# Attention scores with queries on partitions: row maxima and exponentials read from PSUM, probabilities transposed on TensorE

## The chip, the cores and the metric

The kernel runs on one NeuronCore of one Trainium2 chip. TensorE (PE) multiplies matrices, VectorE (DVE), ScalarE (ACT) and GpSimd (POOL) work element by element, and SyncE (SP) issues most of the DMAs. Each engine works through its own instruction list in order and waits on semaphores of the others. The metric is the device time of one execution in microseconds (us); lower is better. A change of about 0.2% is what measurements of this kernel can tell from none.

## The reference

One layer of an encoder on 256 prompt tokens and 1024 sample tokens: two branches (latent attention and a bidirectional retention), a gated merge, then an MLP. All in float32. The change touches the softmax attention, which has 8 heads, with 64 + 32 channels for the scores and 64 for the values:

```python
def block(args):
    qn, qr = args
    s = (jnp.einsum('bqhd,bkhd->bhqk', qn, k_nope)
         + jnp.einsum('bqhd,bkd->bhqk', qr, k_rope))
    p = jax.nn.softmax(s.astype(jnp.float32) * scale, axis=-1).astype(v.dtype)
    return jnp.einsum('bhqk,bkhd->bqhd', p, v)
...
a = mla_attention(q_nope, q_rope, k_nope, k_rope, v_a) @ w_branch_a
```

Prompt and sample tokens attend only among themselves, so a query has 256 or 1024 keys.

## The kernel before

All products are made in a split form: a float32 operand is written as a rounded high part (`split`, L55: a copy on ACT) and a low part (the difference, on DVE or POOL), and one product is three matmuls, high by high, high by low, low by high (`mm3`, L60). PSUM has eight banks of 128 x 512 floats, all taken from one pool (`psum`, L82). A scheduling layer lays the instructions of each engine out in one fixed order before the program is built; the order in which the code asks for work is its starting point.

The program goes through five stages: input projections, retention, attention (`phase_attn`, L640), merge (`phase_merge`) and MLP. During attention TensorE also has the gate projections to do, 16 x 3 groups of 8 products from the resident `hT` (generator `gates`, L646). They depend on nothing in the attention, and are dealt out between its steps as filler: `fill` (L792) takes as many as the share of attention done asks for, out of a total of `TOTF`; `PRE` (33) of them come ahead of the first scores, `ENDF` and `EL` are spent in the last rounds, and what is left runs at the start of the merge (`prep_o`, L842).

Attention is cut into 40 units, (head, 256 queries, all their keys): per head one unit with 2 key blocks of 128 and four with 8. The scores stand with keys on partitions and queries along the row. For a unit with 8 key blocks:

- `qk` (L697): 24 matmuls of 256 columns (the key block is the stationary operand), copied from PSUM into the SBUF tile `s` by ACT (L706).
- `kmax` (L709): DVE takes the maximum over the 8 key blocks, 2048 elements per partition (L711). `qmax1` (L714): two 128 x 128 transposes on TensorE and a second maximum on DVE (L720), `mc`. `qmax2` (L724): two more transposes (L727) spread the maximum of each query over all partitions, in PSUM.
- `soft` (L731): DVE subtracts it from `s` (L740), ACT takes the exponential (L742) and the high part `eh`; the low part `el` is made half by POOL, half by DVE. POOL adds up the blocks (L748) for the sums.
- `sums` (L755): two matmuls with a vector of ones finish the row sums, which go to DRAM (`l_s`).
- `av` (L764): 16 matmuls of 256 columns multiply with the values; DVE copies the result (L779) and SP stores it to `a_s`.

The main loop (L806) runs these as a pipeline over units: in one round the scores of unit i, the value product of unit i-3, the maxima of unit i-1, and so on. In the merge, `prep_a` (L1140) loads `l_s`, inverts it and stores `r_s`, from which the normalisation is broadcast. `load_o` (L857) loads the retention output into the tiles `ot`, which are transposed at the start of the merge (L104) before the first products with `w_branch_b`, whose raw weights come through `wload` (L145). `load_k` (L677) has one buffer: the keys of the next head are split once the last scores of this head are done.

Of the kernel before, what the change touches and what calls it, by code (L numbers as in the profile page):

```python
# [18 lines left out]
P = 128  # L19
# [19 lines left out]
TOTF = 13.25  # L39
ENDF = 8  # L40
PRE = 33
FA = 0.25
EB = (3, 5, 6, 7)
EL = 4
CK = 12
# [3 lines left out]
class Build:  # L49
# [104 lines left out]
    def build(self):  # L154
# [20 lines left out]
        self.l_s = d("l_s", [HEADS, T])  # L175
# [464 lines left out]
    def phase_attn(self):  # L640
# [47 lines left out]
        def load_q(u):  # L688
            h, s0, ns, q0 = u
            qraw = sp.tile([P, 256], F32, tag="qraw", name="qraw", bufs=1)  # L690
            nc.sync.dma_start(out=qraw, in_=self.q_s[h, :, q0:q0 + 256])
            qh = sp.tile([P, 256], F32R, tag="qh", name="qh")
            ql = sp.tile([P, 256], F32R, tag="ql", name="ql")
            self.split(qh, ql, qraw)
            return qh, ql

        def qk(u, q, k):  # L697
            h, s0, ns, q0 = u
            s = sp.tile([P, 8, 256], F32, tag="s", name="s", bufs=3)
            for i in range(0, ns, 2):  # L700
                ps = self.psum()
                for x in range(2):
                    kc = slice((s0 + i + x) * P, (s0 + i + x + 1) * P)
                    self.mm3(ps[:, x * 256:(x + 1) * 256], (k[0][:, kc], k[1][:, kc]), q,
                             True, True)
                nc.scalar.copy(s[:, i:i + 2], ps.rearrange("p (u n) -> p u n", u=2))  # L706
            return s

        def kmax(u, s):  # L709
            mx = sp.tile([P, 256], F32, tag="mx", name="mx")  # L710
            nc.vector.tensor_reduce(mx, s[:, 0:u[2]].rearrange("p k q -> p q k"), AX.X, ALU.max)  # L711
            return mx

        def qmax1(mx):  # L714
            ps = self.psum()
            for x in range(2):
                nc.tensor.transpose(out=ps[:, x * P:(x + 1) * P], in_=mx[:, x * P:(x + 1) * P],
                                    identity=self.ident)
            mc = sp.tile([P, 2], F32, tag="mc", name="mc")
            nc.vector.tensor_reduce(mc, ps[:, 0:256].rearrange("p (x k) -> p x k", x=2), AX.X,  # L720
                                    ALU.max)
            return mc

        def qmax2(mc):  # L724
            pb = self.psum()
            for x in range(2):
                nc.tensor.transpose(out=pb[:, x * P:(x + 1) * P],  # L727
                                    in_=mc[:, x:x + 1].broadcast_to([P, P]), identity=self.ident)
            return pb[:, 0:256]

        def soft(u, s, ma):  # L731
            h, s0, ns, q0 = u
            st = min(ns, 4)
            es = []
            for i in range((ns + 3) // 4):
                eh = sp.tile([P, 4, 256], F32R, tag="eh", name="eh", bufs=4)
                el = sp.tile([P, 4, 256], F32R, tag="el", name="el", bufs=4)
                es.append((eh, el))
                sv = s[:, 4 * i:4 * i + st]
                nc.vector.tensor_tensor(sv, sv, ma.unsqueeze(1).broadcast_to([P, st, 256]),  # L740
                                        ALU.subtract)
                nc.scalar.activation(sv, sv, AF.Exp, scale=SCALE)  # L742
                self.split(eh[:, 0:st], el[:, 0:st], sv, nc.vector if i else nc.gpsimd)
            n, src = ns, s
            t = sp.tile([P, 4, 256], F32, tag="t", name="t", bufs=1)
            while n > 1:
                n //= 2
                nc.gpsimd.tensor_tensor(t[:, 0:n], src[:, 0:n], src[:, n:2 * n], ALU.add)  # L748
                src = t
            sh = sp.tile([P, 256], F32R, tag="sh", name="sh", bufs=3)  # L750
            sl = sp.tile([P, 256], F32R, tag="sl", name="sl", bufs=3)
            self.split(sh, sl, t[:, 0])
            return es, (sh, sl)

        def sums(u, e):  # L755
            h, s0, ns, q0 = u
            pl = self.psum()[0:2, 0:256]
            for i in range(2):
                nc.tensor.matmul(pl, lhsT=one, rhs=e[1][1 - i], start=i == 0, stop=i == 1)
            lt = gt.tile([1, 256], F32, tag="lt", name="lt", bufs=1)  # L760
            nc.vector.tensor_copy(lt, pl[0:1])
            nc.sync.dma_start(out=self.l_s[h:h + 1, q0:q0 + 256], in_=lt)

        def av(u, v, e):  # L764
            h, s0, ns, q0 = u
            j = h % 2
            po = self.psum()[:, 0:256]
            for i in range(ns):
                eh, el = e[0][i // 4]
                if i == ns - 1:  # L770
                    nc.tensor.matmul(po[0:VD], lhsT=v[:, s0 + i, j, 0:VD], rhs=el[:, i % 4],
                                     start=False, stop=False)
                nc.tensor.matmul(po, lhsT=v[:, s0 + i, j], rhs=eh[:, i % 4], start=i == 0,
                                 stop=i == ns - 1)
                if i < ns - 1:
                    nc.tensor.matmul(po[0:VD], lhsT=v[:, s0 + i, j, 0:VD], rhs=el[:, i % 4],
# [29 lines left out]
        for i in range(nu + 4):  # L806
            if i + 1 < nu:
                q[i + 1] = load_q(units[i + 1])
# [687 lines left out]
```

## Time and profile before

| | us |
|---|---|
| median of 3 runs | 2189.68 (2186.43 to 2190.81) |
| the profiled execution, its own time | 2190.64 |
| its span in the trace | 2188.9 |

The profile is of that one execution. It names, for each engine, when an instruction ran, for how long, and what it had waited for. A matmul's duration includes the time until its result is in PSUM, and the next starts before it has ended; so what a matmul costs TensorE in a row of them is the distance from one start to the next, not its duration.

### The profile page before, as it was taken

What the parts mean: (1) busy time and instruction counts of PE and PEld (TensorE: products, weight loads), DVE (VectorE), ACT (ScalarE), POOL (GpSimd) and SP (SyncE); (2) the same over time, 40 slices, a digit from 0 to 9 for tenths busy, and PEclk for the clock granted to TensorE, in tenths of its full rate; (3) what the DMA queues carried; (4) which work ended last, traced back from release to release, by engine and by line L of the source; (5) the groups of instructions that cost most, each with busy time, mean ns of one, the idle gap of its engine ahead of it and who ended that gap; (6) DMA issues with size and microseconds to landing.
All of it is one profiled execution on the core that took longest, in us unless ns stands there. A gap on an engine that the chain in (4) does not pass through costs nothing.

```text
span 2188.9 us, 32539 instructions
## 1 busy us (share of the span) xinstructions
PE 2075.1 (95%) x11856; PEld 1802.5 (82%) x11856; DVE 1407.4 (64%) x2803; ACT 933.1 (43%) x1901; POOL 759.7 (35%) x574
## 2 busy tenths in 40 slices
PE   7899999999988899889899999799999989999998
PEld 6888989888977788777788899688888878878886
DVE  7744646464689898988423618765555545994558
ACT  6422222222366566566323524444444434433442
POOL 1212121211046566566224710244434414970110
PEclk8999999999999999999999999899999999999999
DMA  3351111110222323221554504143343357533444
GB/s 146 111 202 31 53 39 44 39 45 20 89 77 67 89 76 90 66 70 45 198 159 145 193 21 154 57 153 124 129 148 138 129 192 270 173 91 96 141 148 150
DMA packets 169569, 241.10 MB, mean 110 GB/s; under 512 B 15768, under 2 KB 104768, under 8 KB 169408
## 3 DMA queue, kind: packets, MB, share of 16 engines
q1 hardware_dynamic: 161408, 230.82, 32.4%
q10 hardware_dynamic: 8000, 8.20, 1.1%
q8 instruction: 93, 1.52, 0.3%
q14 instruction: 68, 0.56, 0.1%
HBM read 159.91 MB, written 79.05 MB: 109 GB/s over the span
## 4 chain that ended last, share of the span: by engine, by line
PE 73%; DVE 10%; issue 6%; ACT 4%; DMA 4%; POOL 3%; SPq 0%; DVEq 0%; ACTq 0%; POOLq 0%
PE ps L63 22%; PE ps L65 22%; PE ps L64 22%; POOL t L748 2%; ACT s L706 1%; DVE el L58 1%; PE ps L540 1%; PE ps L543 1%; DVE s L740 1%; DVE mx L711 1%; ACT s L742 1%; PE ps L521 1%; PE ps L586 1%; PE ps L585 1%; DVE ql L58 1%
## 5 line engine op out<-in xcount | busy, mean ns | idle before, releaser
L63 PE MATMUL ps<-wh,uh 128*128 128x512 f32 x550 | 209.3, 393 | 8.4 <-ACT wh L57 5.8
L64 PE MATMUL ps<-wl,uh 128*128 128x512 f32 x550 | 215.7, 392 | 0.0
L65 PE MATMUL ps<-wh,ul 128*128 128x512 f32 x550 | 215.1, 392 | 0.0
L58 DVE TENSOR_TENSOR ul<-ur,uh 128x640 fp32r<-128x640 f32 x110 | 123.8, 1125 | 114.4 <-ACT uh L57 114.3
L57 ACT CAST uh<-ur 128x640 fp32r<-128x640 f32 x110 | 80.4, 731 | 211.7 <-PE ps L64 168.1
L748 POOL TENSOR_TENSOR t<-s 128x1024 f32<-128x1024 f32 (+1 forms) x40 | 91.9, 2297 | 167.6 <-ACT s L742 109.7
L711 DVE TENSOR_REDUCE mx<-s 128x256 f32<-128x2048 f32 (+1 forms) x40 | 130.4, 3260 | 23.4 <-ACT s L706 23.2
L1203 POOL TENSOR_TENSOR a<-a 128x640 f32<-128x640 f32 x64 | 85.3, 1343 | 169.7 <-ACT a L1227 73.2
L63 PE MATMUL ps<-hTh,wgh 128*128 128x512 f32 (+1 forms) x384 | 141.5, 368 | 2.5 <-ACT s L706 1.6
L64 PE MATMUL ps<-hTl,wgh 128*128 128x512 f32 (+1 forms) x384 | 138.3, 360 | 0.0
L65 PE MATMUL ps<-hTh,wgl 128*128 128x512 f32 (+1 forms) x384 | 138.1, 360 | 0.0
L63 PEld LDWEIGHTS ps<-wh,uh 128*128 128x128 f32 x550 | 104.1, 189 | 31.0 <-ACT wh L57 9.2
L63 PE MATMUL ps<-wah,hTh 128*128 128x512 f32 x320 | 127.9, 400 | 0.0
L65 PE MATMUL ps<-wah,hTl 128*128 128x512 f32 x320 | 125.0, 391 | 0.0
L64 PE MATMUL ps<-wal,hTh 128*128 128x512 f32 x320 | 124.7, 390 | 0.0
L64 PEld LDWEIGHTS ps<-wl,uh 128*128 128x128 f32 x550 | 104.3, 190 | 22.4 <-DVE wl L58 0.6
L65 PEld LDWEIGHTS ps<-wh,ul 128*128 128x128 f32 x550 | 104.2, 190 | 21.7
L63 PE MATMUL ps<-h2h,feh 128*128 128x512 f32 (+1 forms) x352 | 117.8, 337 | 1.4 <-ACT h2h L57 1.4
L64 PE MATMUL ps<-h2l,feh 128*128 128x512 f32 (+1 forms) x352 | 118.5, 337 | 0.0
L58 POOL TENSOR_TENSOR el<-s,eh 128x1024 fp32r<-128x1024 f32 (+1 forms) x40 | 95.0, 2374 | 67.3 <-ACT eh L57 67.3
L65 PE MATMUL ps<-h2h,fel 128*128 128x512 f32 (+1 forms) x352 | 118.1, 337 | 0.0
L500 DVE TENSOR_TENSOR t<-ps,rcs 128x256 f32<-128x256 f32 x40 | 17.0, 424 | 154.0 <-ACT v L494 136.6
(343 smaller groups left out, 6582.7 us busy)
## 6 DMA issues: line engine op xcount, KB each, us to landing
u_s<-a SPq DMA_DIRECT2D x112, 320.0 KB
ur<-u_s SPq DMA_DIRECT2D x112, 320.0 KB
uraw<-w_up SPq DMA_DIRECT2D x32, 512.0 KB
wd<-w_down SPq DMA_DIRECT2D x64, 256.0 KB
wraw<-w_in SPq DMA_DIRECT2D x24, 512.0 KB
x<-xs SPq DMA_DIRECT2D x16, 512.0 KB
g_s<-g SPq DMA_DIRECT2D x32, 256.0 KB
sg<-g_s SPq DMA_DIRECT2D x32, 256.0 KB
```

The costliest lines, as they stand in the source:

```text
L57: nc.scalar.copy(hi, src)
L58: (eng or nc.vector).tensor_tensor(lo, src, hi.bitcast(F32), ALU.subtract)
L63: mm(out, lhsT=lh, rhs=rh, start=start, stop=False, skip_group_check=more)
L64: mm(out, lhsT=lh, rhs=rl, start=False, stop=False, skip_group_check=more)
L65: return mm(out, lhsT=ll, rhs=rh, start=False, stop=stop, skip_group_check=more)
L521: nc.tensor.transpose(out=pT[:, i * P:(i + 1) * P], in_=qkf[:, i * P:(i + 1) * P], identity=self.ident)
L540: nc.tensor.matmul(ps2[j][:, 0:P], lhsT=qkT[r, 256:384], rhs=qkT[r, j * P:(j + 1) * P], start=True, stop=True)
L543: nc.tensor.matmul(ps2[j][:, P:256], lhsT=ddf[:, j * P:(j + 1) * P], rhs=v[:, j * P:(j + 1) * P], start=True, stop=True)
L585: nc.tensor.matmul(po[:, c], lhsT=sv[:, c], rhs=v[:, c], start=True, stop=False)
L711: nc.vector.tensor_reduce(mx, s[:, 0:u[2]].rearrange("p k q -> p q k"), AX.X, ALU.max)
L748: nc.gpsimd.tensor_tensor(t[:, 0:n], src[:, 0:n], src[:, n:2 * n], ALU.add)
L1203: nc.gpsimd.tensor_tensor(r[:, s], r[:, s], r[:, s], ALU.mult)
```

## The change

Scores now stand with queries on partitions and keys along the row. A unit is worked off in two steps of 128 queries (`x` = 0, 1):

- `qk`: the queries are stationary; with 8 key blocks two PSUM banks of 512 keys, three 512-column matmuls each (two key blocks: one bank, 256 columns). DVE takes the maximum of each bank along the row, from PSUM; one small DVE instruction combines them into `nm`, minus the scaled maximum; ACT takes exp(scale * score + nm) straight from PSUM into `p`, and adds up the row at the same time into `ls`.
- `turn`: eight (or two) 128 x 128 transposes of `p` on TensorE into two PSUM banks (or one); ACT makes `eh` and DVE makes `el` from there.
- `av` is as before. `kmax`, `qmax1`, `qmax2`, `soft` and `sums` go, and so do `l_s` and its inversion in `prep_a`: after the last unit the sums of all heads are inverted in one instruction, transposed once and stored to `r_s`.

The constants that place the filler differ, and `qraw` and `at` have two buffers.

```diff
-TOTF = 13.25
-ENDF = 8
-PRE = 33
-FA = 0.25
+TOTF = 13.4
+ENDF = 6
+PRE = 24
+FA = 0.2
 EB = (3, 5, 6, 7)
-EL = 4
-CK = 12
+CK = 4
...
-            qraw = sp.tile([P, 256], F32, tag="qraw", name="qraw", bufs=1)
+            qraw = sp.tile([P, 256], F32, tag="qraw", name="qraw", bufs=2)
...
-        def qk(u, q, k):
+        def qk(u, x, q, k):
             h, s0, ns, q0 = u
-            s = sp.tile([P, 8, 256], F32, tag="s", name="s", bufs=3)
-            for i in range(0, ns, 2):
+            qs = slice(x * P, (x + 1) * P)
+            w = min(4, ns) * P
+            nb = ns * P // w
+            mx = sp.tile([P, 2], F32, tag="mx", name="mx", bufs=3)
+            pss = []
+            for i in range(nb):
+                ps = self.psum()[:, 0:w]
+                kc = slice(s0 * P + i * w, s0 * P + (i + 1) * w)
+                self.mm3(ps, (q[0][:, qs], q[1][:, qs]), (k[0][:, kc], k[1][:, kc]), True, True)
+                nc.vector.tensor_reduce(mx[:, i:i + 1], ps, AX.X, ALU.max)
+                pss.append(ps)
+            nm = sp.tile([P, 1], F32, tag="nm", name="nm", bufs=3)
+            nc.vector.tensor_scalar(nm, mx[:, 0:1], mx[:, nb - 1:nb], -SCALE, ALU.max, ALU.mult)
+            p = sp.tile([P, D], F32, tag="p", name="p", bufs=3)
+            r = h * NT + q0 // P + x
+            for i in range(nb):
+                nc.scalar.activation(p[:, i * w:(i + 1) * w], pss[i], AF.Exp, scale=SCALE, bias=nm,
+                                     accum_out=ls[:, r, i:i + 1])
+            return p
+
+        def turn(u, x, p, e):
+            h, s0, ns, q0 = u
+            st = min(4, ns)
+            for i in range(0, ns, st):
                 ps = self.psum()
-                for x in range(2):
-                    kc = slice((s0 + i + x) * P, (s0 + i + x + 1) * P)
-                    self.mm3(ps[:, x * 256:(x + 1) * 256], (k[0][:, kc], k[1][:, kc]), q,
-                             True, True)
-                nc.scalar.copy(s[:, i:i + 2], ps.rearrange("p (u n) -> p u n", u=2))
-            return s
-
-        def kmax(u, s):
...
-        def sums(u, e):
...
+                for j in range(st):
+                    nc.tensor.transpose(out=ps[:, j * P:(j + 1) * P],
+                                        in_=p[:, (i + j) * P:(i + j + 1) * P],
+                                        identity=self.ident)
+                hi, lo = (z[:, i:i + st, x * P:(x + 1) * P] for z in e)
+                self.split(hi, lo, ps[:, 0:st * P].rearrange("p (k n) -> p k n", k=st))
...
+        for n in range(ns_ + 3):
+            if n < ns_:
+                i, x = steps[n]
                 u = units[i]
...
+                p = qk(u, x, q[i], k)
+                if x == 1:
+                    q.pop(i)
+                    if i + 1 < nu and units[i + 1][0] != u[0]:
+                        k = load_k(units[i + 1][0])
+                fill(0.5 * x + FA, i)
+            else:
                 for _ in range(ENDF):
                     next(git, 0)
...
+            if prev:
+                i1, x1, p1 = prev
+                if x1 == 0:
+                    es[i1] = [sp.tile([P, 8, 256], F32R, tag=g, name=g) for g in ("eh", "el")]
+                turn(units[i1], x1, p1, es[i1])
+            if n < ns_:
+                fill(0.5 * x + 0.5, i)
+            if old and old[1] == 1:
+                i2 = old[0]
+                av(units[i2], v, es.pop(i2))
...
+        lt = sp.tile([P, HEADS * NT], F32, name="lt", bufs=1)
+        nc.vector.tensor_tensor(lt, ls[:, :, 0], ls[:, :, 1], ALU.add)
+        nc.vector.reciprocal(lt, lt)
+        pl = self.psum()[0:HEADS * NT, 0:P]
+        nc.tensor.transpose(out=pl, in_=lt, identity=self.ident)
+        lr = sp.tile([HEADS * NT, P], F32, name="lr", bufs=1)
+        nc.scalar.copy(lr, pl)
+        nc.sync.dma_start(out=self.r_s.rearrange("h (t p) -> (h t) p", p=P), in_=lr)
...
-        nc.sync.dma_start(out=l, in_=flat(self.l_s))
-        nc.vector.reciprocal(l, l)
-        nc.sync.dma_start(out=flat(self.r_s), in_=l)
```

The lines of the changed kernel have other numbers: `mm3` is L62 to L64, `split`'s low part L57, the maximum L706, `nm` L709, the exponential L713, the transposes of `p` L723, `av` L736 to L744, `load_o` L832, `wload` L144, `to_T` L103.

How the change moves the work on TensorE, around one step of a unit with 8 key blocks. A `wgh` or `wgl` row is filler, `ident` a transpose. Before, at the maxima:

```order
L776 MATMUL ps<-el,v 64x256
L771 MATMUL ps<-el,v 64x256
L773 MATMUL ps<-eh,v 128x256
L64 MATMUL ps<-hTl_88,wgh 128x512
L65 MATMUL ps<-hTh_87,wgl 128x512
L759 MATMUL ps<-sl,one 2x256
L759 MATMUL ps<-sh,one 2x256
L727 MATMUL ps<-ident,mc 128x128 x2
L63 MATMUL ps<-qh,kh 128x256
L64 MATMUL ps<-ql,kh 128x256
L65 MATMUL ps<-qh,kl 128x256
```

The same place now:

```order
L62 MATMUL ps<-hTh_86,wgh 128x512
L63 MATMUL ps<-hTl_87,wgh 128x512
L64 MATMUL ps<-hTh_86,wgl 128x512
L723 MATMUL ps<-ident,p 128x128 x8
L62 MATMUL ps<-hTh_86,wgh 128x512
L63 MATMUL ps<-hTl_87,wgh 128x512
L64 MATMUL ps<-hTh_86,wgl 128x512
L62 MATMUL ps<-hTh_86,wgh 128x512
L63 MATMUL ps<-hTl_87,wgh 128x512
L64 MATMUL ps<-hTh_86,wgl 128x512
L62 MATMUL ps<-kh,qh 128x512
L63 MATMUL ps<-kl,qh 128x512
```

The sums and the spread of the maximum are gone; a run of eight transposes stands between filler, two products of filler before the next scores.

VectorE over about one unit. Before:

```order
L720 TENSOR_REDUCE mc<-ps 128x2
L711 TENSOR_REDUCE mx<-s 128x256
L58 TENSOR_TENSOR ql<-qraw,qh 128x256
L58 TENSOR_TENSOR wgl<-wraw,wgh 128x1024
L761 COPY lt<-ps 1x256
L740 TENSOR_TENSOR s<-s,ps 128x1024 x2
L58 TENSOR_TENSOR el<-s,eh 128x1024
```

Now:

```order
L706 TENSOR_REDUCE mx<-ps 128x1 x2
L709 TENSOR_SCALAR nm<-mx 128x1
L57 TENSOR_TENSOR el<-ps,eh 128x4x128 x2
L706 TENSOR_REDUCE mx<-ps 128x1 x2
L57 TENSOR_TENSOR ql<-qraw,qh 128x256
L709 TENSOR_SCALAR nm<-mx 128x1
L57 TENSOR_TENSOR el<-ps,eh 128x4x128 x2
L744 COPY at<-ps 128x256
```

The long maximum and the two subtractions are gone; all that is left are instructions of 512 columns and less.

SyncE's queue from the end of attention into the merge. Before:

```order
L762 DMA l_s<-lt 1x256
L781 DMA a_s<-at 64x256 x2
L762 DMA l_s<-lt 1x256
L859 DMA ot<-o_s 128x1024 x4
L1145 DMA l<-l_s 128x80
L145 DMA wraw<-w_branch_b 128x4x256 x2
L662 DMA g_s<-g 128x512
L859 DMA ot<-o_s 128x1024 x4
```

Now, first the start of attention and then the same place:

```order
L670 DMA vraw<-v_s 128x5x128
L689 DMA qraw<-q_s 128x256 x2
L832 DMA ot<-o_s 128x1024 x4
L681 DMA kraw<-k_s 64x640
L689 DMA qraw<-q_s 128x256
```

```order
L810 DMA r_s<-lr 80x128
L660 DMA g_s<-g 128x256
L660 DMA g_s<-g 128x512
L144 DMA wraw<-w_branch_b 128x4x256 x2
L660 DMA g_s<-g 128x512
L832 DMA ot<-o_s 128x1024 x4
```

The first four loads of `ot` moved from behind the last sums to the start of attention, and the load of `l` that stood ahead of `w_branch_b` is gone. In the whole stretch from the first scores to the first transposes of `ot`, TensorE's list has 717 filler matmuls of 512 columns and 336 of 256 before (720 and 360 now), 816 matmuls of 256 columns for scores (now 384 of 512 and 48 of 256), 544 for values in both, 80 for sums (now none), and 160 transposes in pairs (now 544 of `p`: 64 runs of eight and 16 of two).

## Rows read from the trace of the kernel before

**Rows 1.** The page: busy time of each engine (share of the span, instructions).

```profile
PE 2075.1 (95%) x11856; PEld 1802.5 (82%) x11856; DVE 1407.4 (64%) x2803; ACT 933.1 (43%) x1901; POOL 759.7 (35%) x574
```

**Rows 2.** Stretches: us; busy PE, PEld, DVE, ACT, POOL (instructions); PEclk; DMA share; GB/s.

```profile
200.00:500.00 300.00, 300.00 (x1880) 262.59 (x1879) 173.20 (x738) 80.58 (x261) 48.90 (x90) 1.00 0.16 46
590.00:1054.00 464.00, 413.28 (x2654) 363.67 (x2652) 399.99 (x379) 280.75 (x444) 272.22 (x144) 0.97 0.26 75
1053.00:1071.00 18.00, 12.14 (x75) 11.07 (x75) 9.63 (x14) 8.45 (x14) 0.00 (x0) 0.81 1.02 368
```

**Rows 3.** Waits of PE in attention: who waited, for whom: total us, times, longest.

```profile
PE ps L727 <- DVE mc L720: 17.3, 10, 3.7
PE ps L776 <- DVE el L58: 8.7, 6, 2.8
```

**Rows 4.** Timeline of PE (start, duration): first and last of 31, 19 and 14 matmuls.

```profile
579.13 0.39 PE L64 MATMUL ps<-hTl,wgh 128*128 128x512 f32 x1
...
585.93 0.39 PE L64 MATMUL ps<-hTl,wgh 128*128 128x512 f32 x1
...
573.07 0.28 PE L64 MATMUL ps<-hTl,wgh 128*128 128x256 f32 x1
...
575.23 0.28 PE L64 MATMUL ps<-hTl,wgh 128*128 128x256 f32 x1
...
807.80 0.28 PE L773 MATMUL ps<-eh,v 128*128 128x256 f32 x1
...
809.32 0.28 PE L773 MATMUL ps<-eh,v 128*128 128x256 f32 x1
```

**Rows 5.** Timeline of PE: transposes and the two matmuls behind them.

```profile
805.33 0.38 PE L717 MATMUL ps<-ident,mx 128*128 128x128 f32 x2
805.46 0.36 PE L63 MATMUL ps<-hTh,wgh 128*128 128x256 f32 x1
805.66 0.28 PE L64 MATMUL ps<-hTl,wgh 128*128 128x256 f32 x1
...
1069.96 1.03 PE L104 MATMUL ps<-ident,ot 128*128 128x128 f32 x8
1070.76 0.37 PE L63 MATMUL ps<-oTh,w8h 128*128 128x256 f32 x1
1070.96 0.28 PE L64 MATMUL ps<-oTl,w8h 128*128 128x256 f32 x1
```

**Rows 6.** Groups by line and shape: count, busy us, mean ns, idle before.

```profile
L711 DVE TENSOR_REDUCE mx<-s 128x256 f32<-128x2048 f32 x32 | 124.9, 3902 | 23.3 <-ACT s L706 23.2
L720 DVE TENSOR_REDUCE mc<-ps 128x2 f32<-128x256 f32 x40 | 16.4, 409 | 1.2 <-PE ps L717 1.2
L706 ACT COPY s<-ps 128x512 f32<-128x512 f32 x136 | 72.5, 593 | 38.6 <-POOL t L748 17.2 <-DVE el L58 14.4 <-PE ps L776 4.2
L1191 DVE TENSOR_TENSOR a<-V,ps 128x512 f32<-128x512 f32 x48 | 33.0, 687 | 64.9 <-PE ps L65 64.8
```

**Rows 7.** Single lines, ns min/median/max: a square with row sums, the query split.

```profile
L1373 ACT ACTIVATE jk<-acc x20: 616/632/660, 1901.2 to 2180.0; 128x512 f32<-128x512 f32 x20
L1373 ACT ACTIVATION_READ_ACCUMULATOR jk<-acc x20: 184/186/218, 1901.7 to 2180.5; 128x1 f32 x20
L58 DVE TENSOR_TENSOR ql<-qraw,qh x40: 403/432/2574, 590.2 to 994.6; 128x256 fp32r<-128x256 f32 x40
```

**Rows 8.** Timeline: the first query of attention; the start of the merge.

```profile
589.31 0.40 ACT L57 CAST qh<-qraw 128x256 fp32r<-128x256 f32 x1
...
1054.45 1.96 PE L104 MATMUL ps<-ident,ot 128*128 128x128 f32 x16 [1.37 <-DMA ot<-o_s]
...
1062.53 0.52 PE L63 MATMUL ps<-oTh,w8h 128*128 128x256 f32 x1 [2.97 <-ACT w8h L57]
```

**Rows 9.** One transpose's duration, ns: min/median/max (instructions of line 104).

```profile
L104 PE MATMUL ps<-ident,ot x80: 270/273/421, 1054.4 to 1082.7; 128*128 128x128 f32 x80
```

More of the change, by code (lines that the diff above doesn't have):

```diff
@@ L709, in kmax @@
-        def kmax(u, s):
[L710 to L753, printed above, removed]
@@ L755, in sums @@
-        def sums(u, e):
[L756 to L762, printed above, removed]
+            qs = slice(x * P, (x + 1) * P)
+            w = min(4, ns) * P
+            nb = ns * P // w
@@ L802, in phase_attn @@
             next(git)
-        one = self.small.tile([P, 2], F32R, name="one", bufs=1)
-        nc.gpsimd.memset(one.bitcast(F32), 1.0)
-        p1 = p2 = p3 = p4 = None
-        for i in range(nu + 4):
-            if i + 1 < nu:
-                q[i + 1] = load_q(units[i + 1])
-            if i < nu:
-                u = units[i]
-                s = qk(u, q.pop(i), k)
-                if i + 1 < nu and units[i + 1][0] != u[0]:
-                    k = load_k(units[i + 1][0])
-                fill(FA, i)
-            elif i < nu + 2:
+        ls = sp.tile([P, HEADS * NT, 2], F32, name="ls", bufs=1)
@@ new lines, in phase_attn @@
+        nc.gpsimd.memset(ls, 0.0)
+        steps = [(i, x) for i in range(nu) for x in range(2)]
+        ns_ = len(steps)
+        prev = old = None
+        es = {}
+        for n in range(ns_ + 3):
+            if n < ns_:
+                i, x = steps[n]
+                u = units[i]
+                if x == 0 and i + 1 < nu:
+                    q[i + 1] = load_q(units[i + 1])
+                p = qk(u, x, q[i], k)
[5 more added lines that the diff above has]
+            else:
@@ L816, in phase_attn @@
                 for _ in range(ENDF):
                     next(git, 0)
-            if p3:
-                av(p3[0], v, p3[1])
-                if p2 and p2[0][0] // 2 != p3[0][0] // 2:
-                    v = load_v(p2[0][0] // 2)
-            if p1:
-                mc = qmax1(p1[2])
-            if i < nu:
-                mx = kmax(u, s)
-                fill(1.0, i)
-            if p4:
-                if i >= nu + 2:
-                    for _ in range(EL):
-                        next(git, 0)
-                sums(*p4)
@@ new lines, in phase_attn @@
+            if old and old[1] == 1:
+                i2 = old[0]
+                av(units[i2], v, es.pop(i2))
+                if i2 + 1 < nu and units[i2 + 1][0] // 2 != units[i2][0] // 2:
+                    v = load_v(units[i2 + 1][0] // 2)
+            old = prev
+            prev = (i, x, p) if n < ns_ else None
+        lt = sp.tile([P, HEADS * NT], F32, name="lt", bufs=1)
+        nc.vector.tensor_tensor(lt, ls[:, :, 0], ls[:, :, 1], ALU.add)
+        nc.vector.reciprocal(lt, lt)
+        pl = self.psum()[0:HEADS * NT, 0:P]
```

19 lines of the change are left out of this document (5 added, 14 removed).

## The prediction

> **What bounds the kernel now.** I read the page first: TensorE is busy for 95% of the span [rows 1], so time is won only where it stands idle, works at a lower clock, or is given less to do. Then the table of stretches shows where that is. In retention it is busy for all of 300 us at full clock; from the first scores to the first transposes of the merge it is busy for 413.28 of 464 us, at a mean granted clock of 0.97, while VectorE is busy for 399.99 and GpSimd for 272.22 [rows 2]. So attention is the stage, and VectorE the engine it leans on. The table of waits says at which link: the longest in total is L727, the transposes that spread the maximum, which waited 17.3 us for `mc`, the maximum on VectorE; next is `av` waiting for `el`, 8.7 us [rows 3].
>
> A busy share flatters TensorE, since a matmul's duration has a tail that the next one overlaps. So I count its work by the distance of starts. 30 distances of 512-column matmuls take 6.80 us, 0.227 each; 18 of 256-column filler 2.16 us, 0.120 each; 13 of `av` 1.52 us, 0.117 each [rows 4], which I use for scores and sums too. A pair of transposes takes 0.13 us to the next start, and the matmul behind it 0.20 instead of 0.12: 0.21 a pair. A run of eight takes 0.80 and the same 0.08 behind it: 0.88 [rows 5]. With the counts of the instruction lists, the stretch of 464 us holds 717 x 0.227 = 162.5 and 336 x 0.120 = 40.3 of filler, 1440 x 0.117 = 168.5 of scores, values and sums, and 80 pairs x 0.21 = 16.8: together 388.1 us. **75.9 us are lost there**, to idling, to the lower clock and to gaps.
>
> **The change part by part.** *Work of TensorE.* Filler is the same in sum. Scores go from 816 x 0.117 = 95.5 us to 384 x 0.227 + 48 x 0.117 = 92.7. Sums (80 x 0.117 = 9.4) and the pairs (16.8) go. The transposes of `p` come: 64 runs of eight x 0.88 = 56.3 and 16 pairs x 0.21 = 3.4, together 59.7. Values stay. That makes 418.8 us, **30.7 more than before**, all of it on the engine that sets the end. The change pays only if the lost 75.9 us shrink by more.
>
> *Load of the others.* Per unit with 8 key blocks, VectorE loses the maximum of 3902 ns [rows 6] and the subtractions. It gets four maxima over 128 x 512 from PSUM and four `el` of that size. The nearest row for both is the 128 x 512 operation on PSUM at 687 ns; a 128 x 256 maximum from PSUM took 409 [rows 6]. For the maximum the bounds are 0.6 (409 ns and the growth of a row twice as long) and 0.98 (a quarter of the 3902); I take 0.69. With two `nm` at 0.41 at most, `at` at 0.41 and `ql` at 0.43 [rows 6, 7] that is 8 x 0.69 + 1.66 = 7.2 us. ScalarE has four exponentials with row sums, each like the square with row sums, 632 + 186 ns [rows 7], four high parts at 593 [rows 6], `qh` at 0.4 [rows 8] and about one copy of filler: 6.6 us. TensorE needs per such unit 12 x 0.227 of scores, 2 x 0.88 of transposes, 16 x 0.117 of values and, by its list, some 24 x 0.227 of filler: 11.8 us. So VectorE and ScalarE are loaded to about 60%. That is the 173.20 of 300 us that VectorE has in retention, where TensorE is busy throughout [rows 2]. GpSimd has nothing to do in the loop. `ql`, whose median is 432 ns and whose longest took 2574 [rows 7], should then stay at the former.
>
> *The new chain and its cover.* From a step's last score to its transposes the list puts two products of filler (1.36), the eight transposes of the step before (0.88), two more of filler, every other time `av` (1.87), the next step's scores (1.36) and filler again: 6.3 us or more. The chain needs the second bank's maximum (0.69), `nm` (0.41), and the exponentials (0.82 each): 1.9 us to the first four transposes, 2.7 to the last. Queued ahead of the exponentials on ScalarE stand at most two high parts, 1.2 us. `av` comes a whole step after the last `el` it reads. PSUM holds at most two banks of scores, two of transposes, one or two of filler and one of values, of eight. So a step of 8 key blocks should run almost without waiting; I put 0.1 us on each of 64, 7 us, between 0 and 0.44 (a rival, below, takes over there).
>
> *What is still lost.* At the start the first query is ready at 589.7 [rows 8], loaded no earlier than before, but nine products of filler fewer stand ahead of it (24 x 0.120 + 3 x 0.227 = 3.6 us), and the first chain (2.4) has little cover: 6 us. When the head changes, keys are split only after the last scores, and the next scores follow after a step of half the former length: seven times 1 us, between 0 and the longest wait shown, 3.7 [rows 3]. For the lower clock and the gaps I keep 6: the 0.97 over 464 us is 14 us now [rows 2], and it follows the idling. Sum: **26 us lost instead of 75.9**.
>
> *Start of the merge.* Between 1053 and 1071 the clock is 0.81 and TensorE is busy for 12.14 of 18 us [rows 2]; it waits 1.37 us for the first `ot`, and 2.97 for the split of `w_branch_b` [rows 8], which shares the DMA engines, at 368 GB/s, with four loads of `ot` of 0.5 MB just ahead of it. These four now land during attention, and the load of `l` ahead of `w_branch_b` on SyncE's queue is gone. I take both waits as saved: 4.3 us, between 0 and 7 (both waits and the clock lost there). The single transposition of the sums, the inversion and the store of `r_s` lie beside the last 13 us of filler. The four loads at the start, 2 MB at that rate, 5.7 us, stand ahead of the third query, which is due some 14 us later, so I cost them at nothing; without that cover they cost those 5.7.
>
> *Sum.* 2190.6 (the profiled execution) - 75.9 + 26 + 30.7 - 4.3 = 2167.1. That execution is 1.0 above the median of 2189.7, so against the median **2166 us**.
>
> **The rivals.** (a) *TensorE as full as in retention.* Same loads on the others, and no wait left in the steps: 11 us lost, 2151. For it speaks the 300 of 300 [rows 2]; against it the start and the seven changes of head, which retention does not have.
>
> (b) *The loss is not softmax's.* If head changes, loads and the clock make most of the 75.9, some 50 remain and the 30.7 are just paid: 2190, no change. Against it: the two longest waits are for `mc` and `el` [rows 3].
>
> (c) *Steps wait for their own exponentials.* Before, a unit's maxima had a round of two steps' length to pass; now a step has half of it, and TensorE's transposes stand in order in front of filler and the next scores. If a maximum from PSUM took the 0.98 and exponentials much over 0.82, or if high parts and filler copies on ScalarE stood ahead of them, each long step would wait. It turns slower than before at 0.44 us more per long step (28 / 64); at 1 us, with 64 us more, it gives 2230. Against it are 3.6 us of slack; for it, that 30.7 us of work leave less room than any wait seen.
>
> (d) *Transposes cost their duration.* If each kept TensorE for the 273 ns it lasts [rows 9], 64 x 8 and 16 x 2 of them took 149 us instead of 59.7, and the time were 2255. Against it are the runs of eight with 0.80 us from the first start to the next matmul [rows 5], that is 0.10 each. The Trainium skill, "TensorE: Matmul & The Clock Gate", Part 4 on the PE-mode transpose, gives about 275 ns for one in a kernel and reminds that a copy out of PSUM follows. By that figure as a price the sum would be that of (d), and the rule speaks against transposing all probabilities; the row agrees with it as a duration and not as a cost in a run.
>
> **How the numbers follow.** Forecast 0.62, (a) 0.14, (b) 0.10, (c) 0.12, (d) 0.02. The predicted time is the forecast's. For the range: with 10 us lost and 7 saved in the merge it is 2148; with 52 lost and nothing saved there 2196. That takes in (a) and (b) and leaves out most of (c), (d) and the tails. Measurements tell 0.2% (4.4 us) from no change, that is faster below 2185.3 and slower above 2194.1: faster 0.62 + 0.14 + a fifth of (b) = 0.78; same 0.08, the rest of (b); slower 0.12 + 0.02 = 0.14.
>
> **What would show it.** Right: the stretch from the first scores to the first transposes of `ot` falls from 464 to about 445 us; the waits for `mc` are gone and no wait of the transposes of `p` for the exponential exceeds a few us in sum; VectorE is busy for some 60% of the stretch and GpSimd for nothing; runs of eight transposes stand 0.80 to 0.88 apart; the first product with `w_branch_b` waits under 1 us; the clock is near 1.0. Wrong: a row "transposes of `p` wait for ACT `p`" with 30 us or more (c); long waits at each change of head for the split keys (b); matmuls behind transposes that start over 0.3 us late, or a lower clock throughout the stretch.

## The result, and the profile after

The changed kernel takes **2156.78 us** (median; 2154.59 to 2158.0) against 2189.64: a ratio of 0.9851, with a 95% interval from 0.9840 to 0.9862. The forecast was 2166, between 2148 and 2196, and faster. Its profiled execution took 2154.59 us at a span of 2152.7.

The page's first part, as in [rows 1]:

```profile
PE 2088.3 (97%) x11777; PEld 1811.3 (84%) x11777; DVE 1259.9 (59%) x2908; ACT 887.6 (41%) x2014; POOL 485.9 (23%) x430
```

The stretch from the first scores to the first transposes of `ot`, and the start of the merge (columns as in [rows 2]):

```profile
586.30:1015.20 428.90, 426.16 (x2601) 374.65 (x2602) 252.20 (x485) 235.29 (x556) 0.00 (x0) 1.00 0.29 83
1015.20:1023.00 7.80, 6.03 (x45) 5.56 (x44) 6.24 (x10) 6.49 (x11) 0.00 (x0) 0.91 0.83 289
```

The stretch fell from 464 to 429 us. TensorE idled for 51 us of it before [rows 2] and idles for 2.7 now, at a mean granted clock of 1.00 (the full 2.4 GHz) instead of 0.97. VectorE is busy for 59%, GpSimd for nothing. All waits of TensorE from the filler to the merge (us, times, longest). Before there were sixteen kinds, 50.5 us in sum, 42.8 of them for VectorE, with those of [rows 3] at their head; now there are two, and neither is for VectorE:

```profile
PE ps L62 <- ACT qh L56: 3.1, 1, 3.1
PE ps L723 <- ACT p L713: 2.7, 2, 2.5
```

Starts in the two timelines cut the program into five stretches:

| stretch, us | before | after | change | forecast |
|---|---|---|---|---|
| up to the first filler | 572.5 | 569.2 | -3.4 | 0 |
| first filler to first scores | 17.4 | 17.2 | -0.3 | 0 |
| first scores to transposes of `ot` | 464.5 | 428.9 | -35.6 | -19.2 |
| to the first product with `w_branch_b` | 8.1 | 4.7 | -3.4 | -4.3 |
| to the last instruction | 1126.3 | 1132.8 | **+6.4** | 0 |

So two things had to be explained: why the attention gained 16 us more than forecast, and why 6 us were lost behind it, in code that the change does not touch. The largest part of that loss lies in the products with `w_out`. The instructions of one of their lines (count, duration min/median/max in ns, first and last start), in the kernel before and then in the changed one:

```profile
L63 PE MATMUL ps<-w8h,mTh x320: 276/276/387, 1237.3 to 1351.6; 128*128 128x256 f32 x160
```

```profile
L62 PE MATMUL ps<-w8h,mTh x320: 278/281/385, 1195.6 to 1316.1; 128*128 128x256 f32 x160
```

The same 960 matmuls, in the same order, at a granted clock of 1.00 in both, took 114.3 us from the first to the last start before and 120.5 after: 0.119 and 0.126 us each over the whole row, 0.1140 and 0.1202 without its interruptions.

### The profile page after: what moved, and what is told of

Read it like the earlier page. It is cut to its first block, busy times and chain, and to the rows that moved or that the text cites. A ratio compares the mean times of both kernels' runs of the same rounds, so it can differ in the third digit from the quotient of the medians.

```text
span 2152.7 us, 32299 instructions
## 1 busy us (share of the span) xinstructions
PE 2088.3 (97%) x11777; PEld 1811.3 (84%) x11777; DVE 1259.9 (59%) x2908; ACT 887.6 (41%) x2014; POOL 485.9 (23%) x430
## 4 chain that ended last, share of the span: by engine, by line
PE 88%; DVE 6%; DMA 2%; ACT 1%; issue 1%; POOL 1%; SPq 0%; DVEq 0%; ACTq 0%; POOLq 0%
PE ps L62 26%; PE ps L64 26%; PE ps L63 26%; PE ps L723 3%; PE ps L738 1%; PE ps L741 1%; PE ps L538 1%; PE ps L541 1%; DVE wl L57 1%; DVE ul L57 1%; DMA sg<-g_s 1%; PE ps L584 1%; PE ps L583 1%; PE ps L519 1%; DVE mb L911 0%
## 5 line engine op out<-in xcount | busy, mean ns | idle before, releaser
L62 PE MATMUL ps<-wh,uh 128*128 128x512 f32 x550 | 210.6, 392 | 7.6 <-ACT wh L56 5.9
L64 PE MATMUL ps<-wh,ul 128*128 128x512 f32 x550 | 214.7, 391 | 0.0
L57 DVE TENSOR_TENSOR ul<-ur,uh 128x640 fp32r<-128x640 f32 x110 | 125.9, 1145 | 111.6 <-ACT uh L56 111.5
L57 DVE TENSOR_TENSOR el<-ps,eh 128x512 fp32r<-128x512 f32 (+1 forms) x144 | 91.9, 656 | 90.2 <-ACT eh L56 90.0
L62 PE MATMUL ps<-hTh,wgh 128*128 128x512 f32 (+1 forms) x384 | 141.2, 368 | 0.0
L64 PE MATMUL ps<-hTh,wgl 128*128 128x512 f32 (+1 forms) x384 | 137.7, 358 | 0.0
L62 PEld LDWEIGHTS ps<-wh,uh 128*128 128x128 f32 x550 | 103.8, 189 | 29.8 <-ACT wh L56 8.4
L62 PE MATMUL ps<-wah,hTh 128*128 128x512 f32 x320 | 128.0, 400 | 0.0
L713 ACT ACTIVATE p<-ps,nm 128x512 f32<-128x512 f32 (+1 forms) x144 | 94.7, 664 | 77.5 <-DVE nm L709 77.3
L64 PE MATMUL ps<-wah,hTl 128*128 128x512 f32 x320 | 125.0, 391 | 0.0
L1125 POOL TENSOR_TENSOR ar<-ar 128x512 f32<-128x512 f32 (+1 forms) x12 | 13.3, 1107 | 487.9 <-DMA ar<-a_s 481.7
L64 PEld LDWEIGHTS ps<-wh,ul 128*128 128x128 f32 x550 | 103.8, 189 | 21.6
L62 PE MATMUL ps<-h2h,feh 128*128 128x512 f32 (+1 forms) x352 | 117.7, 337 | 1.4 <-ACT h2h L56 1.4
L64 PE MATMUL ps<-h2h,fel 128*128 128x512 f32 (+1 forms) x352 | 118.2, 336 | 0.0
L57 DVE TENSOR_TENSOR wl<-wd,wh 128x512 fp32r<-128x512 f32 x110 | 114.7, 1042 | 0.9 <-ACT wh L56 0.9
```

Of the source, the lines that this page charges most:

```text
L57: (eng or nc.vector).tensor_tensor(lo, src, hi.bitcast(F32), ALU.subtract)
L62: mm(out, lhsT=lh, rhs=rh, start=start, stop=False, skip_group_check=more)
L64: return mm(out, lhsT=ll, rhs=rh, start=False, stop=stop, skip_group_check=more)
L713: nc.scalar.activation(p[:, i * w:(i + 1) * w], pss[i], AF.Exp, scale=SCALE, bias=nm, accum_out=ls[:, r, i:i + 1])
```

## The experiments

### Is the loss behind attention a matter of addresses?

In the changed kernel the pool of small tiles is 352 bytes smaller (`one` and `l` are gone), and all tiles on the left side of SBUF lie that much lower: `hT`, the gate weights, and later the merge's weights `w8`; those on the right side, `mT` and `oT`, lie where they did. Three kernels have an unused tile in that pool and otherwise the lists of the kernel that they come from:

```diff
+        pad = self.small.tile([P, 88], F32, name="pad", bufs=1)    # e_pad; 24 in e_pad96
+        pad = self.small.tile([P, 8], F32, name="pad", bufs=1)     # b_pad32, in the kernel before
```

> The changed kernel with 352 bytes more in the pool of small tiles, so that the tiles on the left side of SBUF (normalised input, gate weights, weights of the merge) lie at the addresses that they had in the kernel before; all instruction lists are the same as in the changed kernel. Theory 'addresses': with the same list of matmuls, the stage of the products with w_out took 124.1 us in the changed kernel and 117.9 in the kernel before (distance of starts 0.1202 against 0.1140 us, 952 of them), the products with w_branch_b 0.2342 against 0.2290 (372), those with the low half of the up weights 0.2340 against 0.2296 (215); with the addresses back the w_out stage is at 118 again and the time falls by 6 to 9 us, to about 2149. Rival 'this execution': the distances differ from execution to execution, the w_out stage may be anywhere between 118 and 124, and the median stays within 2 us of 2157.

> The changed kernel with 96 bytes more in the pool of small tiles instead of 352: the tiles of SBUF's left side lie elsewhere than in either kernel, but at the same place within 128 bytes as in the kernel before; all lists are the same. Theory 'place within 128 bytes': the w_out stage takes 117 to 118.5 us again (distance 0.114), the products with w_branch_b stand 0.229 apart. Rival 'the addresses as such, or the distance between the tiles': 123.5 to 124.5 us (0.120), 0.234.

> The kernel before with 32 bytes more in the pool of small tiles, which puts the tiles of SBUF's left side at the place within 128 bytes that they have in the changed kernel; all lists are those of the kernel before. Theory 'place within 128 bytes': the w_out stage goes from 117.9 to 124 us, the products with w_branch_b from 0.229 to 0.234, the kernel to about 2198. Rival 'the addresses as such': 117.9 and 2189, no change.

`e_pad` took 2149.6 us (2146.44 to 2151.31), a ratio of 0.9818 (0.9803 to 0.9834) to the kernel before; single runs gave 2146.96 for `e_pad96` and 2191.27 for `b_pad32`. The same line of the products with `w_out` in `e_pad`, `e_pad96` and `b_pad32`, and in `b_halfmax`, a variant of the kernel before further below whose tiles lie where that kernel's do:

```profile
L62 PE MATMUL ps<-w8h,mTh x320: 276/276/384, 1200.6 to 1314.5; 128*128 128x256 f32 x160
```

```profile
L62 PE MATMUL ps<-w8h,mTh x320: 276/276/394, 1196.4 to 1310.5; 128*128 128x256 f32 x160
```

```profile
L63 PE MATMUL ps<-w8h,mTh x320: 277/281/415, 1230.6 to 1352.0; 128*128 128x256 f32 x160
```

```profile
L63 PE MATMUL ps<-w8h,mTh x320: 281/281/387, 1201.7 to 1320.3; 128*128 128x256 f32 x160
```

113.9, 114.1, 121.4 and 118.6 us. From the first product with `w_branch_b` to the last instruction in `e_pad`, `e_pad96` and `b_pad32` it is 1122.3, 1122.1 and 1134.0: with the old place within 128 bytes the changed kernel wins 10.5 us there, with the new one the kernel before loses 7.6. The products with `w_branch_b` go along, 0.2293, 0.2293 and 0.2335 us apart. So the change lost 7 to 10 us by accident (7.2 by the medians of `e_pad` and the changed kernel, 10.5 by their traces; the table's 6.4 is that less 4.0 which the change saved there), and in these products the place within 128 bytes goes with it. Within 64 would do as well: the pads do not tell the two apart.

Three rows keep this from being the whole cause. `b_halfmax` has the addresses and the order of these products of the kernel before, and stands at 0.118 us in the row with `w_out`, though at 0.229 with `w_branch_b`. Of `b_pad32`'s 121.4 us a part is a granted clock of 0.99 in the mean of the row; its matmuls stand 0.1183 us apart without interruptions, less than the changed kernel's. And `b_pad32` came out at 2191 and not at 2198, in part since retention gained 3.4 us: its 256-column products stand 0.1183 us apart (915 of them) and not 0.1220. In the changed kernel, at the same place within 128 bytes, these stand at 0.1216. (The first scores of `b_pad32` start at 584.0, 5.9 us earlier; most of the rest lies ahead of retention, where the profiled execution of the kernel before was late, as the last item of the account below says.) Which relation between the two operands' places is the good one, and what else moves the distance, these runs do not tell.

### What is the start worth?

```diff
-PRE = 24
+PRE = 33          # e_pre; in e_const also TOTF 13.25, ENDF 8, FA 0.25, CK 12
```

> The changed kernel with 33 products of filler ahead of the first scores instead of 24, as in the kernel before. In the changed kernel TensorE waits 3.13 us for the first high part of a query, and 2.55 for the first exponentials. Theory 'cover at the start': the nine products (3.6 us) cover the first wait, the filler is the same in sum and what is missing later has slack (steps' exponentials are ready 3.65 us in the median before their transposes), so the time falls by 2 to 3 us, to about 2154. Rival 'cover is needed later': the first wait goes and waits of the same size come at changes of head or in the last rounds: 2157, no change. Rival 'order': the scheduler moves the transposes nearer to their exponentials, and waits for p sum up to over 5 us: slower.

> The changed kernel with all constants that place the filler as in the kernel before (total 13.25 instead of 13.4, 8 a round at the end instead of 6, 33 ahead instead of 24, share after the scores 0.25 instead of 0.2, a unit's extra cost 12 instead of 4). Theory 'constants are worth nothing beside the reorganised softmax': as with the 33 alone, about 2154, and not above 2159. Rival 'the constants carry part of the gain': with 12 instead of 4, units with two key blocks get nearly twice the filler and those with eight less, so that exponentials of the long steps are late by some tenths of a us: 64 x 0.3 = 19 us slower, about 2175, with a row of transposes of p waiting for p.

> The changed kernel once more, unaltered. In its profiled execution the granted clock stayed at 1.00 behind the 3 us wait for the first query, and four kernels with the same start had 0.76 to 0.79 in the 20 us behind the first scores, at 4.5 us. Theory 'the wait brings the lower clock in some executions and not in others': times lie in two groups some 4 us apart, the median within 2154 to 2159, and 8 to 16 us (0.4 to 0.7%) above the kernel with 33 ahead and the former addresses. Rival 'the clock at the start belongs to the list': the times lie within 2 us of each other.

`e_pre`: 2150.18 us (2149.04 to 2151.64), 0.9827 (0.9812 to 0.9841). `e_const`: 2152.22 (2150.43 to 2153.86), 0.9836. `again`: 2160.01 (2154.47 to 2162.11), 0.9851 (0.9832 to 0.9871). The stretch in `e_pre`:

```profile
588.60:1011.30 422.70, 422.69 (x2575) 371.28 (x2574) 250.88 (x484) 233.23 (x556) 0.00 (x0) 1.00 0.29 84
```

TensorE does not idle at all: the nine products cover the wait for the query, and, since the clock and the cover hold, the exponentials too. The gain of 6.6 us is more than the 2 to 3 expected. Where the rest was, the first 20 us behind the first scores show, in the changed kernel's first profiled execution, in `again` and in `e_pad`:

```profile
586.30:606.30 20.00, 17.44 (x100) 15.01 (x101) 10.74 (x24) 10.53 (x25) 0.00 (x0) 1.00 0.69 210
```

```profile
587.10:607.10 20.00, 17.45 (x84) 15.17 (x85) 8.65 (x20) 10.17 (x24) 0.00 (x0) 0.83 0.63 189
```

```profile
588.50:608.50 20.00, 17.54 (x77) 15.34 (x78) 7.79 (x18) 9.07 (x22) 0.00 (x0) 0.76 0.64 188
```

Behind the same idling of 3 us for the first query and 2.5 for the first exponentials, TensorE ran at the full clock in one execution and at half of it for a while in the others; `e_pad`'s stretch was 433.45 us for 428.91 with the same list, 4.5 us more. `e_pad`'s five times lie in two groups, at 2146.5 and at 2149.6 to 2151.3. `again`'s lie between 2154.5 and 2162.1 less clearly so. The mean granted clock of each execution goes with it: 0.988 in `e_pad`'s two and `again`'s one that are fast, 0.985 to 0.986 in the others. So the theory of two groups is supported, not shown. The other constants add nothing that can be measured: `e_const` lies 2 us above `e_pre`, with overlapping times.

### What does a transpose cost?

```diff
-                for j in range(st):
+                for j in list(range(st)) * 2:
                     nc.tensor.transpose(out=ps[:, j * P:(j + 1) * P],
```

> The changed kernel with every transposition of p made twice, into the same place: 544 more, in runs of 16 (and 4). Theory 'a transpose costs its place in the row': 0.10 us each, 544 x 0.10 = 54 us more, about 2211; TensorE has no idle time in the stretch that could hide it. Rival 'it costs its duration', 273 ns: 149 us more, about 2305. Rival 'hidden': under 10 us more.

2215.4 us, 58.6 above the median of the changed kernel: 0.108 us for each of 544. Its stretch, at 491.32 us, is 58 to 62 longer than those of `e_pad` and of the changed kernel. Rival (d) falls by 90 us. The figure of the Trainium skill, "TensorE: Matmul & The Clock Gate", Part 4, about 275 ns, is the duration here too (272 ns, in the rows below), and not the cost in a row.

### How much slack has a step?

One step in the changed kernel: VectorE's maxima (two of them in the first row) and `nm`, ScalarE's exponentials, and TensorE's transposes, which need the last of these (start, duration):

```profile
626.87 1.39 DVE L706 TENSOR_REDUCE mx<-ps 128x1 f32<-128x512 f32 x2 [0.27 <-PE ps L64]
628.30 0.21 DVE L709 TENSOR_SCALAR nm<-mx 128x1 f32<-128x1 f32 x1
628.60 0.69 ACT L713 ACTIVATE p<-ps,nm 128x512 f32<-128x512 f32 x1 [4.28 <-DVE nm L709]
...
629.85 0.20 ACT L713 ACTIVATION_READ_ACCUMULATOR p<-ps,nm 128x1 f32 x1
...
633.10 1.04 PE L723 MATMUL ps<-ident,p 128*128 128x128 f32 x8
```

The probabilities are complete at 630.05. The transposes start at 633.10, and the fifth, the first to read the second bank, 0.4 later: 3.45 us to spare. Over all 80 steps the median of this is 3.65, and the least, beside 0.05 at the start, 0.06 at one step with two key blocks. To test that this is real slack, GpSimd, which is idle there, was put into the chain:

```diff
+            for j in range(2):                                     # 5 in e_delay5
+                d = gt.tile([P, 512], F32, tag="dl", name="dl", bufs=2)
+                nc.gpsimd.tensor_tensor(d, zero, nm.broadcast_to([P, 512]), ALU.add)
+                nm = d[:, 0:1]
```

> The changed kernel with two additions of 128 x 512 on GpSimd between nm and the exponentials (each adds nothing to nm), so that every step's exponentials come 2.3 to 2.6 us later by GpSimd's 1.1 us for such an addition; the scheduler moves some instructions around it. Theory 'slack': in the trace of the changed kernel the exponentials are ready 3.65 us (median) before the transposes that read them; with 2.3 us later 15 of 80 steps would wait, 11 us in sum, with 2.6 us 18 steps and 16 us: about 2165 to 2175, less where the scheduler moves the transposes back. Rival 'steps wait for their exponentials': what is added to the chain is paid in every step, 80 x 2.4 = 190 us: about 2345. Rival 'nothing': the order absorbs all of it, 2157.

> The same with five additions, 5.5 to 6.5 us. Theory 'slack': over 70 of the 80 steps now wait, and each pays what goes beyond its slack: 157 us for 5.5, 230 us for 6.5, at an unchanged order: 2310 to 2390, less where the scheduler moves the transposes back, and more where the lower clock follows the waits. Rival 'paid in full in every step': 80 x 6 = 480 us, about 2640. Rival 'nothing': 2157 to 2165.

`e_delay2` took 2196.52 us and `e_delay5` 2320.63, that is 40 and 164 more than the changed kernel. In `e_delay2` TensorE's waits for the probabilities, the stretch, and one of the waits:

```profile
PE ps L727 <- ACT p L717: 27.2, 13, 5.3
```

```profile
586.60:1056.50 469.90, 442.54 (x2602) 384.88 (x2603) 263.10 (x485) 238.77 (x556) 174.86 (x160) 0.97 0.26 76
```

```profile
700.89 1.04 POOL L712 TENSOR_TENSOR dl<-zero,dl 128x512 f32<-128x512 f32 x1
701.96 0.48 ACT L717 ACTIVATE p<-ps,dl 128x256 f32<-128x256 f32 x1 [0.73 <-POOL dl L712]
...
702.58 0.44 PE L727 MATMUL ps<-ident,p 128*128 128x128 f32 x2 [2.02 <-ACT p L717]
```

From the end of `nm` to the exponential it is 2.3 us here against 0.1 in the changed kernel, so 2.2 us a step were added, 180 in sum. Of 80 steps 13 wait, not all: the rival that every step pays falls. But 40 us are more than twice what the slack in the list gave. Two things in the rows make up for it, beside the scheduling layer, which placed some 1100 of the stretch's 2601 matmuls otherwise. Seven of the thirteen waits, 18.9 of the 27.2 us, stand at steps with two key blocks, where a head begins and the exponentials come one step's short length after the last ones; and the clock fell to 0.97 in the mean, which is worth some 14 us of the 470. In `e_delay5` it is 107.6 us of waits at 45 steps and a clock of 0.90. The two additions cost a fifth of the delay that they bring in, the five about a third (164 of some 515), and about half as much as the waits themselves comes on top through the clock.

### Do the early loads make the start of the merge?

```diff
-            p = sp.tile([P, D], F32, tag="p", name="p", bufs=3)
+            p = sp.tile([P, D], F32, tag="p", name="p", bufs=8)
```

> The changed kernel with eight buffers for the probabilities p instead of three; nothing uses the five more, but they take the room in which the tiles ot lay, so that the first four loads of ot stand behind the last transposes of p again, as in the kernel before. 26 rows of TensorE's list change, else only SyncE's. Theory 'early loads are worth the start of the merge': the first transposes of ot wait for their load again and the first product with w_branch_b waits 3 us; from the first transposes of ot to the first product it was 8.08 us before and 4.68 in the changed kernel: 3.4 + 1.4 = about 5 us slower than the changed kernel, about 2162. Rival 'w_branch_b is what is late': the wait at the first product does not depend on the loads of ot: within 1.5 us of 2157.

2161.2 us (2158.71 to 2163.51), 0.9875 (0.9855 to 0.9894): as expected by the time, but not by the trace, and the trace decides. SyncE's loads of `ot` and of `w_branch_b`, and TensorE's first transposes and first product:

```profile
1010.60 1.94 SPq L832 DMA_DIRECT2D ot<-o_s  x4
1020.21 0.93 SPq L144 DMA_DIRECT2D wraw<-w_branch_b  x2
...
1020.01 3.65 PE L103 MATMUL ps<-ident,ot 128*128 128x128 f32 x32
...
1024.79 0.39 PE L62 MATMUL ps<-oTh,w8h 128*128 128x256 f32 x1 [1.12 <-ACT w8h L56]
```

The transposes do not wait, and the first product follows 4.78 us behind, as against 4.68. The loads are late, but 9.4 us of filler still follow them, and they stand 9.6 us ahead of the load of `w_branch_b`. In the kernel before it was 4.25 us ahead of their use, and 2.9 ahead of `w_branch_b`:

```profile
1050.20 1.77 SPq L859 DMA_DIRECT2D ot<-o_s  x4
...
1053.11 0.94 SPq L145 DMA_DIRECT2D wraw<-w_branch_b  x2
...
1061.43 1.04 ACT L57 CAST w8h<-wraw 128x1024 fp32r<-128x1024 f32 x1 [1.20 <-DMA wraw<-w_branch_b]
```

The split of `w_branch_b`, for which the first product waits, started there 8.3 us behind the issue of its load. In `e_otlate` it is 3.5, in the changed kernel 3.3:

```profile
1023.69 1.04 ACT L56 CAST w8h<-wraw 128x1024 fp32r<-128x1024 f32 x1 [0.40 <-DMA wraw<-w_branch_b]
```

The 4.4 us by which `e_otlate` is slower lie in the stretch (433.3 us), whose first 20 us had a clock of 0.77, and `again`, at 2160.0, is as slow without this edit. So loading `ot` at the start of attention is worth nothing beside loading it 9.4 us ahead. That the loads no longer stand just ahead of `w_branch_b`'s fits these rows; the load of `l` between them went too, and no run separates the two.

### Was it the maximum, in the kernel before?

```diff
-            nc.vector.tensor_reduce(mx, s[:, 0:u[2]].rearrange("p k q -> p q k"), AX.X, ALU.max)
+            nc.vector.tensor_reduce(mx, s[:, 0:u[2] // 2].rearrange("p k q -> p q k"), AX.X, ALU.max)
```

> The kernel before with the maximum over the first half of a unit's key blocks alone (it leaves out the other half; any number near the maximum serves in a softmax): VectorE has 32 x 1.95 = 62 us less to do, all else stays. Theory 'softmax on VectorE makes the loss': TensorE waits 49 us in the stretch, 25 of them at the transposes of the maximum and its spread; most of these go, with some of the low clock: 15 to 35 us faster than the kernel before, 2155 to 2175. Rival 'the loss is loads, changes of head and the clock': under 5 us faster. Rival 'the next link takes over' (subtraction, exponential, GpSimd's half of el and its sums): waits for mc go and waits for el grow by as much: 5 to 10 us faster.

2156.24 us (2151.41 to 2158.83), 0.9849 (0.9829 to 0.9869): as fast as the changed kernel, without any of it. The stretch, and its longest waits:

```profile
587.60:1022.30 434.70, 405.02 (x2655) 361.24 (x2653) 349.45 (x379) 283.30 (x446) 268.11 (x144) 0.98 0.28 80
```

```profile
PE ps L727 <- DVE mc L720: 15.7, 9, 4.7
PE ps L776 <- DVE el L58: 5.0, 5, 1.4
```

Half of one VectorE instruction per unit, 50 us of its 400, takes 30 us from the stretch. The scheduling layer also placed instructions otherwise (1069 of the stretch's 2653 matmuls stand elsewhere in TensorE's list), so the 30 us belong to the smaller load and the new order together. TensorE's idling goes from 51 to 30 us, and matmuls at the lower clock become fewer. Its waits for VectorE fall from 42.8 to 22.4 us, those for the other engines only from 6.3 to 5.7. The waits for `mc` hardly fall; what goes entirely are waits for the maximum before it and for small instructions that share VectorE with it, of which these were the largest in the kernel before:

```profile
PE ps L717 <- DVE mx L711: 4.3, 5, 2.3
PE ps L773 <- DVE lt L761: 3.4, 2, 2.8
PE ps L717 <- DVE lt L761: 2.9, 2, 2.7
PE ps L759 <- DVE sl L58: 2.4, 1, 2.4
```

So a good part of the loss was softmax's, and VectorE's load its cause. Rival (b) falls by the changed kernel itself, which has the same changes of head and lost some 10 us (below) and not 50. The row of waits named the right engine, but its 17.3 us were neither what the load cost nor what went with it.

### The two gains together

```diff
+PRE = 33
+        pad = self.small.tile([P, 88], F32, name="pad", bufs=1)
```

> The changed kernel with 33 products of filler ahead of the first scores and with the 352 bytes that put the tiles of SBUF's left side back to their former addresses; its lists are those of the run with the 33 alone. Theory 'both gains add, since one lies at the start of attention and one behind it': that run's 2150.2 less the 6.2 us of the w_out stage, 2 of the products with w_branch_b and 1 of the MLP = 2141, between 2139 and 2144. Rival 'they share a cause': about 2149, as each alone.

2141.94 us (2140.87 to 2146.14), 0.9779 (0.9762 to 0.9796) to the kernel before, and 18 below `again` beside it. The gains add: one lies at the start of attention, the other behind it.

## Why the prediction was right, and where it was off

The groups of VectorE, ScalarE and TensorE in the stretch (columns as in [rows 6]):

```profile
L713 ACT ACTIVATE p<-ps,nm 128x512 f32<-128x512 f32 x128 | 87.1, 688 | 71.9 <-DVE nm L709 71.8
L706 DVE TENSOR_REDUCE mx<-ps 128x1 f32<-128x512 f32 x128 | 86.5, 686 | 23.8 <-PE ps L64 23.3
L57 DVE TENSOR_TENSOR el<-ps,eh 128x512 fp32r<-128x512 f32 x128 | 85.2, 685 | 82.7 <-ACT eh L56 82.6
L723 PE MATMUL ps<-ident,p 128*128 128x128 f32 x544 | 74.5, 272 | 2.7 <-ACT p L713 2.7
L713 ACT ACTIVATION_READ_ACCUMULATOR p<-ps,nm 128x1 f32 x144 | 28.8, 200 | 0.0
L709 DVE TENSOR_SCALAR nm<-mx 128x1 f32<-128x1 f32 x80 | 16.6, 209 | 1.1
```

- *The stage and its engine.* Right: of TensorE's waits 42.8 us were for VectorE and none is now, and `b_halfmax` gives 30 us of the stretch for 50 us of VectorE.
- *Durations.* Right: maximum and `el` 686 and 685 ns (0.69 taken), exponential with its sum 888 (818), `nm` 209 (at most 410). VectorE's 59% was forecast as some 60, the slack's 3.65 us as 3.6.
- *Work of TensorE.* Right: 0.108 us a transpose against 0.11, and `e_pre`, which never idles and has the forecast's counts in the stretch (717 and 336 of filler), takes 422.7 us where they give 418.8. The 3.9 over it are gaps.
- *The sum.* Right as added up. The nine products that moved into the stretch (it has 720 and 360 of filler now) are not in the 418.8; they left as much room in front, where the wait for the first query took their place.
- *What is still lost: mis-sized.* 26 us were put down; from the first filler on, 446.1 us less 418.8 of work, 14.0 of filler in front and 3.6 for the nine products leave 9.7. Of its four terms the start held (3.1 + 2.5 = 5.7 for 6); the clock stayed at 1.00 in this execution, and the gaps were 3.9 for the 6 of both. The steps cost 0.2 instead of 7, and the seven changes of head nothing instead of 7: these two terms are the step that was off. Behind the former stands the slack, 3.65 us in the median. The reason for the latter, at the first change, where the low half of the new head's keys and its first scores stand so:

```profile
633.35 0.82 DVE L57 TENSOR_TENSOR kl<-kraw,kh 128x640 fp32r<-128x640 f32 x1
...
637.21 0.28 PE L62 MATMUL ps<-kh,qh 128*128 128x256 f32 x1
```

  Keys come in two pieces, and the first unit of a head reads only the first, which is ready 2.8 to 3.2 us ahead at all seven changes. The forecast's 1 us a head did not ask which piece is read first. Rival (a), at 0.14, was therefore the better picture: it put 11 us as lost, and 2151.
- *Start of the merge.* Its size held (4.3 forecast; 3.4, and the 1.37 of the first wait, which the table has in the stretch). Of its reason half is left: the loads of `ot` no longer stand just ahead of `w_branch_b`'s, which fits the rows, but for that they need not go to the start of attention (`e_otlate`).
- *Not in the sum.* The addresses, 7 to 10 us by the pads, which leave the table's +6.4; and 3.4 us ahead of the first filler, which by their place belong to the profiled execution of the kernel before: there the first product with `wa` starts at 135.4 us, in the changed kernel's and in all twelve runs above at 132.4 to 134.4, `b_pad32` among them, which has its code.

The errors lie on both sides: attention came out 16.7 us better than forecast, the merge's start 0.9 worse, the part behind took 6.4, and the earlier start gave 3.4. That the time lay well within the range is in part luck: without the accident of the addresses it was 2149.6 (`e_pad`) and 2147.0 (`e_pad96`), at the range's lower end of 2148.

## What to carry to other kernels

On a kernel whose TensorE is busy for 95%, look for the engine that it leans on in the stretch where it is not: taking load off VectorE was worth 35 us here although TensorE got 31 us more to do, and a wait's row names the engine, not the price. Before a step's wait is priced, find what is queued between producer and consumer, and which part of a tile the consumer reads. When a change alters any tile's size, compare the distance of matmuls in stages that it does not touch, before the difference is put down to the change.

## What the runs showed of the hardware

- The distance of matmuls can change with where their operands lie in SBUF: with 352 bytes less in a pool the same list ran at 0.1202 us instead of 0.1140 (256 columns) and at 0.2342 instead of 0.2290 (512), and 96 bytes, which restore the place within 128, brought both back. The place is not all: at the kernel before's addresses `b_halfmax` ran the 256-column list at 0.118.
- Behind 3 us of idling, with 2.5 more soon after, TensorE's granted clock was 0.76 to 0.83 in the mean of 20 us in some executions and stayed at 1.00 in others of the same list, a difference of some 4.5 us.
- Transposes in runs of 8 or 16 among filler cost 0.108 us each at 272 ns of duration, and the granted clock of the stretch with 544 of them was 1.00.
